# Feed-forward middle of a hybrid decoder step: parts of 4, 6, 6, 6 hidden tiles, four rotating PSUM tiles, and separate buffers for the second row of weight blocks

## The chip, the cores and the metric

The kernel runs on one core of a Trainium2 chip (trn2). The metric is the device time of one execution in microseconds (us). The engines are TensorE (PE, matmul; PEld is its weight load), VectorE (DVE), ScalarE (ACT), GpSimd (POOL) and SyncE (SP), which issues nearly all transfers. Operands lie in SBUF, matmuls add up in PSUM.

## The reference

One layer of a decoder with 1024 channels: half a feed-forward, a mixing stage (a gated convolution beside attention in dilated windows, then an output projection), half a feed-forward again, and a last norm. There are 512 prompt tokens and 8 sample tokens with caches; the kernel treats them together as T = 520 columns. What the change touches is this:

```
def rmsnorm(x, g):
    y = x * lax.rsqrt(jnp.mean(x * x, axis=-1, keepdims=True) + EPS)
    return y * g

def half_ffn(x, g, w1, w3, w2):          # w1, w3: 1024 x 2816, w2: 2816 x 1024
    h = rmsnorm(x, g)
    return x + 0.5 * ((jax.nn.silu(h @ w1) * (h @ w3)) @ w2)

x = half_ffn(x, *ffn1)
...
x = x + jnp.concatenate([y_c, y_a], axis=-1) @ w_out
x = half_ffn(x, *ffn2)
y = rmsnorm(x, norm_final)
```

All of it is float32.

## The kernel before, in words

**Tiling.** x is held transposed: eight tiles X[0] to X[7] of 128 channels x 520 tokens. A matmul takes a block of weights of 128 x 128 and TH = 260 tokens, half of the columns. Float32 accuracy comes from splitting each operand into a rounded part (hi, in the type float32r) and the rest (lo): `mm3` (L119 to L123) issues three matmuls, hi by xh (L121), hi by xl (L122) and lo by xh (L123). `load_w` (L95 to L110) loads weights into `raw` (a ring of four), rounds them to `hi` on ScalarE (L108) and takes `lo` on VectorE (L109); `hi` and `lo` are rings of three in the pool wp.

**One feed-forward** is `ffn` (L226), called for i = 0 before the mixing stage and for i = 1 behind it. The 22 hidden tiles of 128 are done in parts that CUTS names.

1. `x_operand` (L201) scales X by the gain and splits it: f0h, f0l (f1h, f1l) on ScalarE (L135) and VectorE (L136). Squares are summed in `acc`, and `rstd_rows` (L164) turns the sum into `rbc`, the factor of the norm for each token: rounding rhi (ACT L171), matmuls with ones (L178, L179), rv (DVE L182), a logarithm and an exponential on ScalarE, and three VectorE steps to L187. The products are taken of X without the factor, and multiplied by rbc behind the matmul.
2. The first part, tiles 0 to 3, is made by plain products, `gemm`: gate (w1), up (w3), and hh and hl = the rounded hidden tile and its rest (L299, L300). In the first feed-forward the first three products ("early") come from weights w0 that are loaded with x. Beside them `x_sums` (L337) makes seven sums of x's blocks: f0sh and f0sl (f1sh, f1sl).
3. `down` (L395) multiplies the part's hidden tiles by w2 and adds half of the result to X (L404).
4. The other hidden tiles come two at a time from `pair` (L307). It calls `seven` (L354) for w1 and for w3: Strassen's scheme in Winograd's form, seven products of 12 matmuls in place of eight. seven loads two rows of blocks, ra and rb, makes the sums `ws` of them on VectorE (L363 to L366), and rounds them all (L372, L373): ha, hb, hs and la, lb, ls. Products add up in three places of PSUM: px takes five of them, with a copy by ScalarE to `a` or `b` (L380, L384, L388) after most, py one and pw two. The next product into px waits for the copy of px.
5. After each part `down` follows. In the last part of the second feed-forward `finish` and `give` (L796, L820) make the last norm and the output.

**What sets the order.** Nothing here is ordered by hand: a scheduler orders the instructions of each engine by priority and by what is ready, within the buffers that are there. Each engine then does its own row in order. A ring's buffer can only be written again when its last reader is done: that is how pools set the order. SP's queue issues the loads in program order; a load waits until its buffer is free. The mixing stage has an order of its own (ORDER), and the last step of it is the output projection `out_proj`, two passes of four blocks, which ends in X (L747, L748).

**Pools before.** psM gives two PSUM tiles and psA or psB one more; `psum_tile` (L229) goes round these three. The first sums z and the x operands are in one pool xa, the sums xo in another, both on the right side of SBUF; su holds ws, hs, ls. ra and rb share wp's `raw`, ha and hb its `hi`, la and lb its `lo`.

Of the kernel before, what the change touches and what calls it, by code (L numbers as in the profile page):

```python
# [38 lines left out]
CUTS = (0, 4, 14, 22)  # L39
SPLIT = 4  # L40
# [11 lines left out]
def tile_step(ctx: ExitStack, tc: tile.TileContext, xT, w0, w1a, w3a, w2a, w_in, w_out, w1b, w3b, w2b,  # L52
# [173 lines left out]
    def ffn(i, w1, w3, w2, g, psum, finish=None):  # L226
        turn = [0]
# [8 lines left out]
        def hidden(m):  # L236
            at = m - max(c for c in CUTS if c <= m)
            pool = hids[at >= CUTS[1]]
            Hh[m] = pool.tile([P, T], F32R, name=f"hh{at}", tag=f"hh{at}")
            Hl[m] = pool.tile([P, T], F32R, name=f"hl{at}", tag=f"hl{at}")  # L240
            return Hh[m], Hl[m]

        with ExitStack() as st:
            gu = st.enter_context(tc.tile_pool(name=f"gu{i}", bufs=1, reuse_waits="tile"))
            hids = [st.enter_context(tc.tile_pool(name=f"hida{i}", bufs=1, reuse_waits="tile"))]
            with ExitStack() as sx:
                xo = sx.enter_context(tc.tile_pool(name=f"xo{i}", bufs=1, side="right", reuse_waits="tile"))
                with tc.tile_pool(name=f"xa{i}", bufs=1, side="right", reuse_waits="tile") as xa:
                    early = []

                    def start_x():
                        SP.dma_start(gv, gvec)
                        SP.dma_start(X[0][:, TH:], xT[:, 0, TH:])

                    if i == 0:
                        SP.dma_start(X[0][:, :TH], xT[:, 0, :TH])
                        for k in range(0, KD, 2):
                            if k:
                                SP.dma_start(X[k], xT[:, k])
                            early.append(load_w(w0[k // 2], 6, [slice(0, 3), slice(3, 6)] if not k else None, then=start_x if not k else None))  # L260
                            SP.dma_start(X[k + 1], xT[:, k + 1])
                        SP.dma_start(ident, idm)
                    xh, xl, sums = x_operand(xa, f"f{i}", g, i == 0)

                    def norm_tiles():
                        t = psum_tile()
                        return [t[:, h] for h in range(2)]

                    rstd_rows(norm_tiles, sums, D, rbc)
                    if early:  # L270

                        early, ws = [psum_tile() for _ in range(3)], early
                        for k in range(KD):
                            for e, ps in enumerate(early):
                                hi, lo = (t[:, 3 * (k % 2) + e] for t in ws[k // 2])
                                for h in range(2):
                                    c = slice(h * TH, (h + 1) * TH)
                                    mm3(ps[:, h, :TH], hi, lo, xh[k][:, c], xl[k][:, c], k == 0, k == KD - 1)
                    xs = []
                    for m in range(CUTS[1]):  # L280
                        pp = []
                        a = gu.tile([P, T], F32, name="a", tag="a", bufs=2)
                        b = gu.tile([P, T], F32, name="b", tag="b")
                        for w, t in ((w1, a), (w3, b)):
                            if early:

                                A.activation(halves(t), early.pop(0)[:, :, :TH], AF.Copy)
                                pp.append(halves(t))
                                continue
                            hi, lo = load_w(w[m], KD)  # L290
                            ps = psum_tile()
                            gemm(ps, [(hi, lo, 0, KD)], xh, xl)
                            pp.append(ps[:, :, :TH])
                        V.tensor_tensor(halves(a), pp[0], halves(rbc), ALU.mult)
                        A.activation(a, a, AF.Silu)
                        V.tensor_tensor(halves(b), pp[1], halves(rbc), ALU.mult)
                        V.tensor_tensor(b, b, a, ALU.mult)
                        hh, hl = hidden(m)
                        A.activation(hh, b, AF.Copy)  # L299
                        V.tensor_tensor(hl, b, hh.bitcast(F32), ALU.subtract)  # L300

                        xs.append(x_sums(xo, xa, f"f{i}", g, m))
                    down(w2, 0, CUTS[1], Hh, Hl, psum_tile)
                hids.append(st.enter_context(tc.tile_pool(name=f"hidb{i}", bufs=1, reuse_waits="tile")))
                su = sx.enter_context(tc.tile_pool(name=f"su{i}", bufs=2, side="right", reuse_waits="tile"))

                def pair(m):  # L307

                    at, aw, bt = psum_tile(), psum_tile(), psum_tile()
                    a = gu.tile([P, 4, TH], F32, name="a", tag="a", bufs=2)  # L310
                    b = gu.tile([P, 4, TH], F32, name="b", tag="b")
                    x = seven(su, w1, m, xs, at, aw[:, 0, :TH], a)
                    A.activation(a[:, 0:2], a[:, 0:2], AF.Silu)
                    A.activation(a[:, 3], a[:, 3], AF.Silu, scale=-1.0)
                    A.activation(a[:, 2], x, AF.Silu, scale=-1.0)
                    x = seven(su, w3, m, xs, bt, aw[:, 1, :TH], b)
                    V.tensor_tensor(b[:, 0:2], b[:, 0:2], a[:, 0:2], ALU.mult)
                    V.tensor_tensor(b[:, 3], b[:, 3], a[:, 3], ALU.mult)
                    V.tensor_tensor(b[:, 2], x, a[:, 2], ALU.mult)
                    for r, sign in ((0, 1.0), (1, -1.0)):  # L320
                        hh, hl = (halves(t) for t in hidden(m + r))
                        of = b[:, 2 * r:2 * r + 2]
                        A.activation(hh, of, AF.Copy, scale=sign)
                        if r:
                            V.scalar_tensor_tensor(hl, of, sign, hh.bitcast(F32), ALU.mult, ALU.subtract)
                        else:
                            V.tensor_tensor(hl, of, hh.bitcast(F32), ALU.subtract)

                for c0, c1 in zip(CUTS[1:], CUTS[2:]):
                    for m in range(c0, c1, 2):  # L330
                        pair(m)
                    if c1 < KF:
                        down(w2, c0, c1, Hh, Hl, psum_tile)
# [61 lines left out]
    def down(w2, k0, k1, Hh, Hl, psum_tile, finish=None):  # L395
# [18 lines left out]
        if not finish:  # L414
            return
# [522 lines left out]
```

## Time and profile before

| what | value |
|---|---|
| median of three runs | 1035.67 us (1033.27 to 1036.26) |
| the profiled execution | 1036.0 us |
| its span in the trace | 1034.2 us |
| TensorE busy | 996.0 us, 96% of the span, 7897 matmuls recorded |
| VectorE busy | 726.5 us, 70% |
| ScalarE busy | 505.0 us, 49% |
| mean granted TensorE clock | 0.981 of full speed |
| transfers | 136.62 MB, mean 132 GB/s |

The profiled execution is 1.8 us longer than its span, and all places in the trace are given in us from the span's start. Matmuls overlap in the records: one of 128 x 260 at full clock has a duration of 0.28 us and the next one starts 0.12 us later, so the distance of starts is the measure. In brackets stands how long an engine stood idle before an instruction, and what ended that. The first feed-forward fills the time to about 389 us, the mixing stage that to 641, the second feed-forward the rest.

### The profile page before, as it was taken

To read this page: it belongs to the slowest core of one execution; us is meant where nothing else is said; L and a number is where in the kernel's file an instruction comes from. 1 tells how busy PE (TensorE), PEld (TensorE's weight loads), DVE (VectorE), ACT (ScalarE), POOL (GpSimd) and SP (SyncE) were. 2 spreads that over 40 slices of the span, in tenths; PEclk is the share of its full clock that TensorE was granted. 3 is DMA by queue.
4 is the path that set the end of the run, shared out by engine and by line. 5 is a ranking of instruction groups with operands and counts; after the bars stand their busy time and mean duration, and the time that the engine had idled before them with its cause. 6 is when DMAs were issued, how large, how long until landed. Compare 5 with 4: busy or idle time off the path is not lost.

```text
span 1034.2 us, 19174 instructions
## 1 busy us (share of the span) xinstructions
PE 996.0 (96%) x7897; PEld 965.4 (93%) x7897; DVE 726.5 (70%) x1193; ACT 505.0 (49%) x833; POOL 92.2 (9%) x103
## 2 busy tenths in 40 slices
PE   6999999999999999999999998999999999999997
PEld 5999999999999999999999897999998999999897
DVE  6788888436786546667688799797887634788332
ACT  4534565323555436566565545443555422555342
POOL 1000000000000031112022263000000000000022
PEclk6999999999999999999999999999999999999998
DMA  6325434354443445243246665325334233333302
GB/s 208 113 90 186 144 131 140 105 183 156 148 157 125 143 141 173 83 144 129 66 146 222 205 203 184 103 82 184 133 125 151 64 90 113 102 103 103 101 22 83
DMA packets 37912, 136.62 MB, mean 132 GB/s; under 512 B 5760, under 2 KB 8512, under 8 KB 37312
## 3 DMA queue, kind: packets, MB, share of 16 engines
q1 hardware_dynamic: 37824, 135.39, 39.2%
q8 instruction: 62, 1.02, 0.4%
q14 instruction: 26, 0.21, 0.1%
HBM read 131.07 MB, written 37.82 MB: 163 GB/s over the span
## 4 chain that ended last, share of the span: by engine, by line
PE 70%; DVE 15%; DMA 6%; issue 4%; ACT 4%; POOL 1%; SPq 0%; POOLq 0%; DVEq 0%; ACTq 0%
PE ps L121 22%; PE ps L123 21%; PE ps L122 21%; DVE lo L373 3%; DMA raw<-in_w1b 2%; DVE lo L109 2%; DMA raw<-in_w3b 2%; DVE ls L373 1%; ACT hi L108 1%; PE s L568 1%; DMA raw<-in_w1a 1%; DVE ws L364 1%; DVE raw L365 1%; ACT hi L372 1%; DVE ws L363 1%
## 5 line engine op out<-in xcount | busy, mean ns | idle before, releaser
L108 ACT ACTIVATE hi<-raw 128x1024 fp32r<-128x1024 f32 (+3 forms) x136 | 119.1, 878 | 215.6 <-PE ps L122 167.3
L121 PE MATMUL ps<-hh,hi 128*128 128x260 f32 x704 | 200.5, 287 | 4.3 <-ACT hi L108 3.5
L123 PE MATMUL ps<-hh,lo 128*128 128x260 f32 x704 | 200.8, 286 | 1.5 <-DVE lo L109 1.4
L122 PE MATMUL ps<-hl,hi 128*128 128x260 f32 x704 | 199.9, 285 | 0.5 <-DVE hl L300 0.3
L109 DVE TENSOR_TENSOR lo<-raw,hi 128x1024 fp32r<-128x1024 f32 (+3 forms) x136 | 143.6, 1057 | 74.9 <-ACT hi L108 74.0
L121 PEld LDWEIGHTS ps<-hh,hi 128*128 128x128 f32 x704 | 133.5, 191 | 6.8 <-ACT hi L108 4.3
L123 PEld LDWEIGHTS ps<-hh,lo 128*128 128x128 f32 x704 | 134.0, 190 | 3.0 <-DVE lo L109 2.5
L122 PEld LDWEIGHTS ps<-hl,hi 128*128 128x128 f32 x704 | 134.0, 190 | 1.2 <-DVE hl L300 1.2
L121 PE MATMUL ps<-mh,hi 128*128 128x260 f32 x384 | 110.3, 288 | 1.8 <-DVE q L498 1.1
L123 PE MATMUL ps<-mh,lo 128*128 128x260 f32 x384 | 109.3, 285 | 0.3 <-DVE u L619 0.3
L122 PE MATMUL ps<-ml,hi 128*128 128x260 f32 x384 | 109.4, 285 | 0.0
L372 ACT ACTIVATE hi<-raw 128x1024 fp32r<-128x1024 f32 x72 | 75.7, 1053 | 60.8 <-PE ps L122 58.2
L144 POOL TENSOR_TENSOR acc<-acc,sq 128x520 f32<-128x520 f32 (+1 forms) x25 | 38.3, 1530 | 752.9 <-ACT sq L143 748.8
L373 DVE TENSOR_TENSOR lo<-raw,hi 128x1024 fp32r<-128x1024 f32 x72 | 87.5, 1217 | 4.8 <-ACT hi L372 4.8
L372 ACT ACTIVATE hs<-ws 128x1024 fp32r<-128x1024 f32 x72 | 60.5, 840 | 54.0 <-DVE ws L364 48.0
L121 PE MATMUL ps<-f1sh,hi 128*128 128x260 f32 x288 | 82.1, 285 | 3.4 <-DVE X L404 1.2
L121 PE MATMUL ps<-f0sh,hi 128*128 128x260 f32 x288 | 82.2, 286 | 2.0 <-ACT a L384 1.7
L122 PE MATMUL ps<-f0sl,hi 128*128 128x260 f32 x288 | 81.4, 283 | 0.0
L123 PE MATMUL ps<-f1sh,lo 128*128 128x260 f32 x288 | 80.2, 282 | 1.3 <-DVE lo L373 1.2
L122 PE MATMUL ps<-f1sl,hi 128*128 128x260 f32 x288 | 81.3, 283 | 0.0
L123 PE MATMUL ps<-f0sh,lo 128*128 128x260 f32 x288 | 79.6, 282 | 0.0
L404 DVE SCALAR_TENSOR_TENSOR X<-ps,X 128x260 f32<-128x260 f32 x96 | 36.7, 422 | 57.9 <-PE ps L123 57.9
(278 smaller groups left out, 2744.8 us busy)
## 6 DMA issues: line engine op xcount, KB each, us to landing
out_cko<-in_ck SPq DMA_DIRECT2D x16, 1023.0 KB, 7.1
out_cvo<-in_cv SPq DMA_DIRECT2D x16, 1023.0 KB, 7.2
raw<-in_w_in SPq DMA_DIRECT2D x24, 512.0 KB, 3.3
raw<-in_w1b SPq DMA_DIRECT2D x22, 512.0 KB, 3.3
raw<-in_w3b SPq DMA_DIRECT2D x22, 512.0 KB, 3.3
raw<-in_w3a SPq DMA_DIRECT2D x21, 512.0 KB, 3.3
raw<-in_w1a SPq DMA_DIRECT2D x20, 512.0 KB, 3.3
raw<-in_w2a SPq DMA_DIRECT2D x16, 320.0 KB, 3.0
```

Source lines behind the costliest of these rows:

```text
L108: A.activation(hi, raw, AF.Copy)
L109: V.tensor_tensor(lo, raw, hi.bitcast(F32), ALU.subtract)
L121: PE.matmul(out, lhsT=hi, rhs=xh, start=start, stop=False, skip_group_check=more)
L122: PE.matmul(out, lhsT=hi, rhs=xl, start=False, stop=False, skip_group_check=more)
L123: PE.matmul(out, lhsT=lo, rhs=xh, start=False, stop=stop, skip_group_check=more)
L144: G.tensor_tensor(dst[:, c], dst[:, c], sq[:, c], ALU.add)
L363: V.tensor_tensor(s[:, 0], rb[:, :KQ], rb[:, KQ:], ALU.add)
L364: V.tensor_tensor(s[:, 1], s[:, 0], ra[:, :KQ], ALU.add)
L365: V.tensor_tensor(rb[:, :KQ], rb[:, :KQ], ra[:, :KQ], ALU.add)
L372: A.activation(h, f, AF.Copy)
L373: V.tensor_tensor(l, f, h.bitcast(F32), ALU.subtract)
L404: V.scalar_tensor_tensor(X[m][:, c], ps[:, h, :TH], 0.5, X[m][:, c], ALU.mult, ALU.add)
```

## The change

- **Parts.** CUTS is (0, 4, 10, 16, 22): three groups of three pairs instead of one of five and one of four. There is one more `down` pass, with fewer matmuls in each; the number of matmuls is the same.
- **PSUM.** A fourth tile (pool ps4, tag m4) joins the rotation; it is given back before the last `down`. The two tiles psN of the last norm take its place.
- **Second row of blocks.** rb has a ring of two of its own in su, hb and lb have one buffer each there. wp's rings are left to ra, ha, la and w2.
- **Pools of x.** xo goes to the left side, z has its own pool xz, and xa stands alone on the right.
- **Fewer, larger instructions.** px of w1 and of w3 are the two halves of one PSUM tile; py and pw are the two halves of another and are added by one instruction of 520 columns. The hidden tiles are allocated two at a time, and a pair's product, hh and hl are each one instruction of 1040 columns (two of 520 for the last pair of a part). `down` updates X by one instruction of 520. x_sums merges two subtractions. The sign of the second row is turned earlier (`a[:, 3]` by -1 on VectorE, `b[:, 2]` by a copy on ScalarE).
- **Tail.** Of the last `down` three tiles instead of two are done by halves (TAIL), and SPLIT is 1.

```diff
-CUTS = (0, 4, 14, 22)
-SPLIT = 4
+CUTS = (0, 4, 10, 16, 22)
+TAIL, SPLIT = 3, 1
...
         def psum_tile():
             turn[0] += 1
-            pool, tag = (psum, "m3") if turn[0] % 3 == 0 else (psM, "mm")
+            pools = [(p, "m4") for p in more] + [(psM, "mm"), (psM, "mm"), (psum, "m3")]
+            pool, tag = pools[(turn[0] - 1) % len(pools)]
...
-                xo = sx.enter_context(tc.tile_pool(name=f"xo{i}", bufs=1, side="right", reuse_waits="tile"))
-                with tc.tile_pool(name=f"xa{i}", bufs=1, side="right", reuse_waits="tile") as xa:
+            xo = st.enter_context(tc.tile_pool(name=f"xo{i}", bufs=1, reuse_waits="tile"))
+            more.append(sx.enter_context(tc.tile_pool(name=f"ps4{i}", bufs=1, space=PSUM)))
+            with tc.tile_pool(name=f"xa{i}", bufs=1, side="right", reuse_waits="tile") as xa, \
+                    tc.tile_pool(name=f"xz{i}", bufs=2, side="right", reuse_waits="tile") as xz:
...
+            def pair(m, last):
+                px, pa, pb = psum_tile(), psum_tile(), psum_tile()
...
+                x = seven(su, w1, m, xs, px[:, 0, :TH], pa[:, :, :TH], a)
...
+                x = seven(su, w3, m, xs, px[:, 1, :TH], pb[:, :, :TH], b)
+                hh, hl = (t.rearrange("p r (h n) -> p (r h) n", h=2) for t in hidden(m))
+                A.activation(b[:, 2], x, AF.Copy, scale=-1.0)
+                for of in (slice(0, 2), slice(2, 4)) if last else (slice(0, 4),):
+                    V.tensor_tensor(b[:, of], b[:, of], a[:, of], ALU.mult)
+                    A.activation(hh[:, of], b[:, of], AF.Copy)
+                    V.tensor_tensor(hl[:, of], b[:, of], hh[:, of].bitcast(F32), ALU.subtract)
...
             preload()
+            sx.close()
+            more.clear()
             down(w2, CUTS[-2], KF, Hh, Hl, psum_tile, finish)
...
-    def seven(pool, w, m, xs, ps, pw, out):
+    def seven(pool, w, m, xs, px, pyw, out):
+        py, pw = pyw[:, 0], pyw[:, 1]
-        ra, rb = (wp.tile([P, KD, P], F32, name="raw", tag="raw", bufs=4) for _ in range(2))
+        ra = wp.tile([P, KD, P], F32, name="raw", tag="raw", bufs=4)
+        rb = pool.tile([P, KD, P], F32, name="rb", tag="rb")
...
-        ha, hb = (wp.tile([P, KD, P], F32R, name="hi", tag="whi") for _ in range(2))
-        la, lb = (wp.tile([P, KD, P], F32R, name="lo", tag="wlo") for _ in range(2))
+        ha = wp.tile([P, KD, P], F32R, name="hi", tag="whi")
+        la = wp.tile([P, KD, P], F32R, name="lo", tag="wlo")
+        hb, lb = (pool.tile([P, KD, P], F32R, name=n, tag=n, bufs=1) for n in ("hb", "lb"))
...
         product(px, hb, lb, 2, False)
         A.activation(out[:, 2], px, AF.Copy)
         product(pw, hs[:, 2], ls[:, 2], 1, False)
-        V.tensor_tensor(out[:, 3], out[:, 2], out[:, 3], ALU.add)
+        V.scalar_tensor_tensor(out[:, 3], out[:, 2], -1.0, out[:, 3], ALU.mult, ALU.subtract)
         product(px, hb[:, KQ:], lb[:, KQ:], 5, False)
-        V.tensor_tensor(out[:, 1], pw, out[:, 1], ALU.add)
+        V.tensor_tensor(out[:, 0:2], pyw, out[:, 0:2], ALU.add)
```

Three places show how the rows of the engines change. A number behind a name only tells buffers of one name apart; lines of the changed kernel are one higher here.

TensorE at the first norm: ps_223 to ps_225 are the early products before, ps_229 to ps_231 in the changed kernel; rhi by ones_r is the norm's matmul. Before:

```order
L121 MATMUL ps_224<-f0h5_172,hi_135 128x260
L122 MATMUL ps_224<-f0l5_173,hi_135 128x260
L123 MATMUL ps_224<-f0h5_172,lo_136 128x260
L178 MATMUL ps_209<-rhi_205,ones_r_78 128x260
L121 MATMUL ps_223<-f0h0_150,hi_114 128x260
L122 MATMUL ps_223<-f0l0_151,hi_114 128x260
L123 MATMUL ps_223<-f0h0_150,lo_115 128x260
```

With the change:

```order
L122 MATMUL ps_231<-f0h7_186,hi_149 128x260
L123 MATMUL ps_231<-f0l7_187,hi_149 128x260
L124 MATMUL ps_231<-f0h7_186,lo_150 128x260
L179 MATMUL ps_215<-rhi_211,ones_r_78 128x260
L122 MATMUL ps_480<-f0h0_156,hi_475 128x260
```

Before, the norm's matmul stands behind 36 matmuls of one early product and ahead of the other two products; now it stands behind all 144 matmuls of the three, and a later product follows it.

ScalarE at the end of the output projection, where the second feed-forward's operand f1h is made from X (hi is a rounding of weights, sq a square). Before:

```order
L143 ACTIVATE sq_7514<-X4_68 128x520
L108 ACTIVATE hi_7547<-raw_7546 128x1024
L143 ACTIVATE sq_7517<-X5_69 128x520
L108 ACTIVATE hi_7602<-raw_7601 128x1024
L143 ACTIVATE sq_7520<-X6_70 128x520
L108 ACTIVATE hi_7678<-raw_7677 128x1024
L135 ACTIVATE f1h0_7472<-X0_64,gv_74 128x520
L135 ACTIVATE f1h1_7476<-X1_65,gv_74 128x520
```

With the change:

```order
L109 ACTIVATE hi_7255<-raw_7254 128x512
L136 ACTIVATE f1h0_7416<-X0_64,gv_74 128x520
L141 ACTIVATE acc_75<-X0_64 128x520
L136 ACTIVATE f1h1_7420<-X1_65,gv_74 128x520
L144 ACTIVATE sq_7449<-X1_65 128x520
L109 ACTIVATE hi_7289<-raw_7288 128x512
L136 ACTIVATE f1h2_7424<-X2_66,gv_74 128x520
```

Before, all eight f1h stand behind the last squares and the roundings of three later tiles of weights; now each stands behind its own X tile, among the roundings for the output projection.

TensorE inside a pair, where the fourth product into px (of hb, the second row) follows the third (of hs). Before, with ps_1253 the px:

```order
L123 MATMUL ps_1253<-f0sh3_728,ls_1272 128x260
L121 MATMUL ps_1255<-f0sh0_389,hi_1384 128x260
L122 MATMUL ps_1255<-f0sl0_390,hi_1384 128x260
L121 MATMUL ps_1253<-f0sh0_389,hi_1267 128x260
L122 MATMUL ps_1253<-f0sl0_390,hi_1267 128x260
```

With the change, with ps_2075 the px:

```order
L122 MATMUL ps_2075<-f0sh3_726,hs_2210 128x260
L123 MATMUL ps_2075<-f0sl3_727,hs_2210 128x260
L124 MATMUL ps_2075<-f0sh3_726,ls_2211 128x260
L122 MATMUL ps_2075<-f0sh0_394,hb_2208 128x260
L123 MATMUL ps_2075<-f0sl0_395,hb_2208 128x260
```

Before, two matmuls of another product stand between the two; at this place of the changed kernel none does.

## Rows read from the trace of the kernel before

**Rows 1.** Page: span, and the granted clock in 40 slices (tenths).

```profile
span 1034.2 us, 19174 instructions
...
PEclk6999999999999999999999999999999999999998
```

**Rows 2.** Stretches: from:to, length, busy us (matmuls) by engine, clock, DMA share, GB/s.

```profile
67.00:92.00 25.00, 24.00 (x194) 23.20 (x193) 18.61 (x34) 8.20 (x12) 0.00 (x0) 1.00 0.57 190
...
205.00:255.00 50.00, 50.00 (x419) 50.00 (x418) 23.68 (x39) 13.38 (x18) 0.00 (x0) 1.00 0.53 175
...
92.00:388.60 296.60, 291.43 (x2377) 287.59 (x2376) 197.95 (x301) 138.15 (x226) 11.96 (x8) 0.99 0.42 143
719.00:1016.00 297.00, 288.44 (x2347) 283.89 (x2346) 191.52 (x294) 138.04 (x226) 9.09 (x6) 0.99 0.31 100
...
641.00:651.00 10.00, 5.25 (x23) 4.85 (x22) 9.96 (x14) 7.07 (x11) 1.53 (x2) 0.66 0.47 159
```

**Rows 3.** TensorE's timeline and its waits (us, times, longest): copies of px.

```profile
118.37 0.28 PE L122 MATMUL ps<-f0sl,hi 128*128 128x260 f32 x1
118.89 0.39 PE L121 MATMUL ps<-f0sh,hi 128*128 128x260 f32 x1 [0.24 <-ACT a L384]
...
PE ps L121 <- ACT a L384: 1.7, 7, 0.2
...
797.58 0.28 PE L123 MATMUL ps<-f1sh,lo 128*128 128x260 f32 x1
798.34 0.39 PE L121 MATMUL ps<-f1sh,hi 128*128 128x260 f32 x1 [0.48 <-ACT a L388]
```

**Rows 4.** TensorE's timeline and stretches: two ends of parts.

```profile
200.11 0.39 PE L121 MATMUL ps<-hh,hi 128*128 128x260 f32 x1 [0.70 <-ACT hi L108]
...
345.16 0.39 PE L121 MATMUL ps<-hh,hi 128*128 128x260 f32 x1 [1.03 <-ACT hi L108]
...
335.00:351.00 16.00, 14.24 (x98) 13.32 (x97) 7.03 (x10) 5.09 (x7) 0.00 (x0) 0.89 0.50 165
347.20:350.50 3.30, 3.30 (x17) 3.30 (x16) 0.00 (x0) 0.00 (x0) 0.00 (x0) 0.50 1.25 459
```

**Rows 5.** Timelines of TensorE, ScalarE and VectorE: start of the second feed-forward.

```profile
640.83 0.28 PE L123 MATMUL ps<-Yh,lo 128*128 128x260 f32 x1
644.02 0.51 PE L121 MATMUL ps<-f1h,hi 128*128 128x260 f32 x1 [2.90 <-ACT f1h L135]
...
643.25 5.05 ACT L135 ACTIVATE f1h<-X,gv 128x520 fp32r<-128x520 f32 x8
...
643.45 1.07 DVE L748 TENSOR_TENSOR X<-X,t 128x520 f32<-128x520 f32 x1
```

**Rows 6.** Timelines of TensorE and VectorE, and one stretch: head and first part.

```profile
23.35 0.58 PE L178 MATMUL ps<-rhi,ones_r 128*128 128x260 f32 x1 [2.17 <-ACT rhi L171]
...
27.84 0.76 DVE L182 TENSOR_SCALAR rv<-ps 128x260 f32<-128x260 f32 x2 [3.81 <-PE ps L179]
...
31.45 0.70 DVE L187 SCALAR_TENSOR_TENSOR rbc<-rq,rbc 128x520 f32<-128x520 f32 x1
...
35.62 1.22 DVE L109 TENSOR_TENSOR lo<-raw,hi 128x1024 fp32r<-128x1024 f32 x1
...
71.53 0.70 DVE L300 TENSOR_TENSOR hl<-b,hh 128x520 fp32r<-128x520 f32 x1 [0.71 <-ACT hh L299]
...
32.10:72.20 40.10, 39.18 (x322) 38.37 (x321) 37.22 (x54) 21.32 (x24) 0.00 (x0) 1.00 0.39 124
```

**Rows 7.** VectorE's waits in 715 to 805, loads (KB, us to landing), one stretch.

```profile
DVE ws L363 <- DMA raw<-in_w3b: 6.7, 4, 2.8
...
raw<-in_w1b SPq DMA_DIRECT2D x22, 512.0 KB, 3.3
...
92.00:190.00 98.00, 96.59 (x792) 95.18 (x791) 80.78 (x122) 55.70 (x97) 0.00 (x0) 1.00 0.42 143
```

More of the change, by code (lines that the diff above doesn't have):

```diff
@@ L238, in hidden @@
             pool = hids[at >= CUTS[1]]
[L239 to L243, printed above, removed]
+            h, l = (pool.tile([P, 2, T], F32R, name=f"h{x}{at}", tag=f"h{x}{at}") for x in "hl")
+            for r in range(2):
+                Hh[m + r], Hl[m + r] = h[:, r], l[:, r]
+            return h, l
+        with ExitStack() as st, ExitStack() as sx:
@@ L244, in ffn @@
             gu = st.enter_context(tc.tile_pool(name=f"gu{i}", bufs=1, reuse_waits="tile"))
             hids = [st.enter_context(tc.tile_pool(name=f"hida{i}", bufs=1, reuse_waits="tile"))]
-            with ExitStack() as sx:
-                xo = sx.enter_context(tc.tile_pool(name=f"xo{i}", bufs=1, side="right", reuse_waits="tile"))
-                with tc.tile_pool(name=f"xa{i}", bufs=1, side="right", reuse_waits="tile") as xa:
[L249 to L333, printed above, removed]
@@ L334, in ffn @@
+            for c0, c1 in zip(CUTS[1:], CUTS[2:]):
+                for m in range(c0, c1, 2):
+                    pair(m, m == c1 - 2)
+                if c1 < KF:
+                    down(w2, c0, c1, Hh, Hl, psum_tile)
             preload()
+            sx.close()
+            more.clear()
             down(w2, CUTS[-2], KF, Hh, Hl, psum_tile, finish)
     def x_sums(pool, tmp, name, col, k):
-        z = tmp.tile([P, 8, TH], F32, name=f"{name}z", tag="z", bufs=2)
+        z = tmp.tile([P, 8, TH], F32, name=f"{name}z", tag="z")
@@ L404, in update, with whole @@
             V.scalar_tensor_tensor(X[m][:, c], ps[:, h, :TH], 0.5, X[m][:, c], ALU.mult, ALU.add)
-        for m in range(KD - 2 if finish else KD):
+        def whole(m):
             ws = parts(m)
@@ L409, in down @@
             gemm(ps, ws, Hh, Hl)
-            for h in range(2):
-                update(m, ps, h)
+            V.scalar_tensor_tensor(halves(X[m]), ps[:, :, :TH], 0.5, halves(X[m]), ALU.mult, ALU.add)
             if finish:
                 finish(m, None)
+        for m in range(KD - TAIL if finish else KD):
+            whole(m)
         if not finish:
             return
-        ws = [parts(m) for m in (KD - 2, KD - 1)]
+        ws = [parts(m) for m in range(KD - TAIL, KD)]
         for h in range(2):
-            ps = psum_tile()
-            gemm(ps, ws[0], Hh, Hl, [h])
-            update(KD - 2, ps, h)
-            finish(KD - 2, h)
+            for m in range(KD - TAIL, KD - 1):
+                ps = psum_tile()
+                gemm(ps, ws[m - KD + TAIL], Hh, Hl, [h])
+                update(m, ps, h)
+                finish(m, h)
             ps = psum_tile()
             if not h:
-                gemm(ps, ws[1], Hh, Hl, [0])
+                gemm(ps, ws[-1], Hh, Hl, [0])
                 update(KD - 1, ps, 0)
@@ L790, in tile_step @@
             out_proj(4, r2)
-    with ExitStack() as st_f, tc.tile_pool(name="psB", bufs=1, space=PSUM, reuse_waits="tile") as psB:
+    with tc.tile_pool(name="psB", bufs=1, space=PSUM, reuse_waits="tile") as psB, ExitStack() as st_f:
         TF = TH // 4
@@ L805, in finish @@
                 part["p"] = st_f.enter_context(tc.tile_pool(name="fp", bufs=1, side="right", reuse_waits="tile"))
+                part["ps"] = st_f.enter_context(tc.tile_pool(name="psN", bufs=1, space=PSUM))
                 part["sq"] = part["p"].tile([P, T], F32, name="fsq")
@@ L808, in finish @@
             c = slice(h * TH, (h + 1) * TH)
-            ps = psB.tile([P, 512], F32, name=f"nps{h}", tag=f"n{h}")
+            ps = part["ps"].tile([P, 512], F32, name=f"nps{h}", tag=f"n{h}")
             A.activation(sq[:, c], X[m][:, c], AF.Square)
@@ L822, in give @@
             fp, c = part["p"], slice(h * TH, (h + 1) * TH)
-            both = [ps, psB.tile([P, 512], F32, name="nps0", tag="n0")] if h else [ps]
+            both = [ps, part["ps"].tile([P, 512], F32, name="nps0", tag="n0")] if h else [ps]
             for p in both:
```

76 lines of the change are left out of this document (64 added, 12 removed).

## Prediction, made before the changed kernel was run

> **What bounds the kernel now.** I read the page's totals first. TensorE's row of clocks is full in nearly all of the 40 slices [rows 1]; the question is therefore not which engine is the bound but where TensorE stands still or runs at half clock. I read that from the table of stretches, by one rule. In 205 to 255 us nothing waits: 419 matmuls touch 50.00 us, two of them at the edges, so one takes 50.00/417 = 0.120 us. Any other stretch has lost its length minus (its matmuls - 2) x 0.120. By that rule the middle of the first feed-forward (92 to 388.6) lost 11.8 us, that of the second (719 to 1016) 15.8 us, the beginning of the second (641 to 651) 7.5 us, and the end of the first feed-forward's first part (67 to 92) 2.0 us [rows 2]. Everything else, the mixing stage above all, is nearly the same on TensorE in both programs. So the change can touch about 37 us in the feed-forwards, besides the head (the first 32 us).
>
> Then I looked at what each loss is. **(a) px.** seven() sums five products in one PSUM tile and copies it to SBUF four times; the next product has to wait for the copy. With two other matmuls put between, the next one starts 0.52 us after its forerunner, with 0.24 idle; seven such waits behind one line are counted in the first feed-forward. With none between, 0.76 us and 0.48 idle [rows 3]. Beyond a pitch, and with 0.1 us for a slow second matmul, that is 0.5 and 0.74 us. **(b) The ends of parts.** There the down product waits for the rounded w2 weights, which wait for a buffer of the ring of three: 0.70 us at 200.11 and 1.03 us at 345.16. After the second the granted clock was 0.50 for 3.3 us (half of 2.4 GHz), after the first it was not; the whole end at 335 to 351 us cost 16.00 - 96 x 0.120 = 4.5 us, the half clock some 3.3/2 = 1.7 of it [rows 4]. **(c) The second start.** The last product of the output projection begins at 640.83, the first of the second feed-forward at 644.02. Its operand f1h was only made in a block of eight from 643.25, although seven of the eight X tiles were done before the last one at 643.45 + 1.07 = 644.5 [rows 5]. **(d) The head.** The norm's matmul starts at 23.35; VectorE reads its result at 27.84 and has rbc at 31.45 + 0.70 = 32.15 (4.3 us later); the last hidden rest of the first part is done at 72.2. Of these 40.1 us VectorE works 37.22: it is the bound there [rows 6].
>
> **The change, part by part** (sums against the profiled execution's 1036.0 us; the median of the runs shown is 1035.67, 0.3 us less).
>
> *A. Head and first part, -1.5 us.* All three early tiles (144 matmuls) stand before the norm's matmul, instead of 36. They can start where the 36 did, at about 8.3. At full pitch the 144 end at 8.3 + 17.2 = 25.5; the sum's rounding stands behind two weight roundings in ScalarE's queue, so the norm is done at about 27 and rbc at 27 + 4.3 = 31.5. If the clock stays at half (0.22 us a matmul) until 26.3, as it did, 86 are done by then, the rest ends at 33.2 and rbc is at 37.4. I take 34. Behind rbc VectorE's list is shorter by three lo subtractions of 1.22 us [rows 6], which now stand ahead of the norm, and about 1.5 us of smaller ones (merged x_sums and one more lo): 40.1 - 5.2 = 34.9. The last rest comes at 66.4 to 72.3, in the middle 68.9. But TensorE has only 30 down matmuls left to do before it, so it idles some us there and I count 1.7 us for a half clock after it; 162 matmuls are left (19.4 us): 68.9 + 1.7 + 19.4 = 90.0, and half of the 2.0 us that this stretch loses now: about 91 against 92.3. Bounds: 66.4 + 19.4 + 1 = 86.8 (-5.5) and 72.3 + 1.7 + 19.4 + 2 = 95.4 (+3).
>
> *B and D. The two middles, +0.8 and -3.2 us.* The number of matmuls is the same (7842 in both programs). With four rotating tiles and one px tile for w1 and w3, the scheduler's order shows, per feed-forward: about five waits inside a group with nothing between (5 x 0.74), one with one and one with two between (0.6 + 0.5): 4.8 us; one end per part where the last products have nothing to be mixed with, three of 1.0 to 1.4 us: 3.4; the first down product waiting for the last pair's rounding, halved by `last`, three times 0.8: 2.4; and lateness of weights, where I put 2, a share of the waits on loads in the second half [rows 7]. Sum 12.6. The wait for w2 [rows 4] is not in it: three of its tiles are rounded before a part ends now, because rb, hb and lb have left the rings. What covers an evacuation now is only a 0.12 us matmul per place; where even that is gone I have priced it at 0.74. 12.6 against 11.8 and 15.8 gives the two terms. The clock is not lost in it, since 0.70 us of waiting kept it. Bounds: the px waits hidden as well as today and ends at 0.7 us: 8 (-4 and -7.2); twelve waits instead of seven, or half clocks at two ends, 3.4 more to 5 more (+5 and +3).
>
> *C. The second start, -5.7 us.* ScalarE now makes each f1h right behind its X tile, so the eight are spread over the output projection; the last is ready near 644.5 + 0.65, its rest near 646, and TensorE has 44 matmuls (5.3 us from 641) that need no f1h7. Of the 7.5 us some 1.8 stay, for the norm and a slow first group. Bounds: 0.2 left (-7.3), or ScalarE's extra work in front of the w_out roundings holding the last output tiles (-3).
>
> *E. Tail, -0.3 us.* Three last tiles by halves with SPLIT 1; the final chain behind the last matmul is unchanged. Bounds 0 and -0.5.
>
> VectorE's instructions fall from 1195 to 1080, ScalarE's rise from 802 to 810; both lie beside matmuls in the middles and I count them at nothing there: in 92 to 190 VectorE works 80.78 of 98.00 us [rows 7]. The 282 transfers are the same.
>
> Sum: -1.5 + 0.8 - 5.7 - 3.2 - 0.3 = -9.9, so 1036.0 - 9.9 = **1026 us**.
>
> **The rivals.**
>
> *More than that, 1012 us.* The early block runs at full clock, and the four tiles hide px: every term at its better bound, -5.5 - 4 - 6.8 - 7.2 - 0.5 = -24. For it: TensorE is dense earlier in the head. Against it: the order shows the bare places. Chance 0.16.
>
> *No change, 1036 us: the clock at the ends of parts.* Six ends with waits of 1.0 to 1.4 us instead of four. Of the two ends shown, the longer wait lost the clock, the shorter one not [rows 4]; if each new end loses it, 6 x 1.7 = 10.2 us eat the gain: 1026 + 10 = 1036. It decides at a wait between 0.70 and 1.03 us at a part's end. For it: my own price of an end is over 1.0. Against: the wait for w2, the cause of both, is gone. The Trainium skill, page "TensorE: Matmul & The Clock Gate", section "A second HAM failure mode: psum-queue depth-cycling", speaks against rotating through banks: a kernel that cycled through PSUM banks had its matmul groups broken by many very short idle times, and its clock swung between both levels. By it the change would lose clock also at the places inside the parts; the trace of before does not bear that out, since px waits of 0.24 and 0.48 us left the mean granted clock of 92 to 388.6 at 0.99 [rows 2]. Chance 0.14.
>
> *Slower, 1044 us: the raw second block is late.* rb has a ring of two and hb, lb one buffer each. The load into an rb can only start when VectorE has read the one before, and takes 3.3 us; VectorE's next instruction in order is the sum that needs it. Today 4 such waits of up to 2.8 us stand in one stretch of the second half [rows 7]. VectorE has 80.78 us of work per 790/168 = 4.7 pairs, 17.2 us a pair, where TensorE needs 168 x 0.120 = 20.2. So it decides at 3.0 us of waiting per pair: at 4.0, 1 us for each of 18 pairs, +18: 1026 + 18 = 1044. For it: an rb of w3 frees only right ahead of the next w1's. Against: VectorE loses over a tenth of its instructions. Chance 0.13.
>
> *The change doesn't do what it says*: the order of f1h shows it does; 0.01.
>
> **How the numbers follow.** My forecast has 0.56, with a range of its own of 1018 to 1034. A measurement of this kernel can tell about 0.3% (3.1 us) from no change. Faster: 0.56 + 0.16, and 0.01 of the rest; same 0.14; slower 0.13. The range goes from 1012 (the larger gain, with about a twentieth below) to 1037 (no change, all but the slower case).
>
> **What would show it.** C: no TensorE idle over 1 us near 641 to 647, and f1h single in ScalarE's row. Ends of parts: no wait on hi at L109, clocks of 1.00 there. Head: rbc near 34 and the last rest near 69. Middles: waits of 0.4 to 0.5 us behind `a` and `b` copies. I am wrong if the six ends show 0.50 clocks, or if VectorE waits on loads of rb by over 3 us a pair.

## The result, and the profile after

The changed kernel takes **1053.32 us** (median of four, 1048.93 to 1054.22) against 1035.97 for the kernel before: ratio 1.0168, 95% interval 1.0141 to 1.0195. It is slower by some 17 us, where 10 us less were forecast. The profiled execution is the quickest of the four, 1048.93 us, 12.9 more than the 1036.0 of before; the other three, at 1052.6 to 1054.2, had a mean granted clock of 0.983 instead of its 0.988. The trace therefore shows 13 of the 17 us.

The page of the changed kernel, the lines that answer to [rows 1]:

```profile
span 1047.2 us, 19070 instructions
...
PEclk9989999999999999999999999999989999999998
```

The stretches, for [rows 2], with the columns as there; the first is the head and the second the end of the first part, the next two are the middles, then the second start, and the last two are the pieces of the middles at half clock:

```profile
4.60:26.10 21.50, 19.03 (x146) 17.86 (x146) 19.54 (x25) 14.01 (x21) 4.22 (x3) 1.00 0.76 271
55.10:88.60 33.50, 27.68 (x197) 26.55 (x196) 27.11 (x38) 12.84 (x15) 0.00 (x0) 0.85 0.60 204
88.60:397.00 308.40, 295.06 (x2376) 288.48 (x2375) 197.04 (x251) 141.71 (x228) 9.70 (x7) 0.99 0.39 130
725.90:1029.70 303.80, 291.19 (x2340) 285.32 (x2339) 189.43 (x243) 140.41 (x228) 6.96 (x6) 0.99 0.28 89
649.70:659.70 10.00, 7.95 (x61) 7.37 (x61) 9.70 (x11) 5.46 (x9) 2.60 (x2) 1.00 0.36 119
123.40:126.80 3.40, 2.99 (x14) 3.00 (x15) 1.63 (x2) 0.95 (x4) 0.00 (x0) 0.50 0.10 35
758.20:765.00 6.80, 6.22 (x27) 5.93 (x28) 5.66 (x9) 4.19 (x7) 0.00 (x0) 0.50 0.23 77
```

By the prediction's rule (length minus matmuls less two, by 50/417 us) the middles now lose 308.4 - 2374 x 50/417 = 23.7 us and 303.8 - 2338 x 50/417 = 23.5 us, where they lost 11.8 and 15.8. Cut behind the last down matmul of each first part, at the places that the rows name, and for the tail at the last norm's first matmul, the spans of both profiles compare like this:

| piece | before | after | difference | forecast |
|---|---|---|---|---|
| head and first part | 91.8 | 88.6 | -3.2 | -1.5 |
| first middle | 296.8 | 308.5 | +11.7 | +0.8 |
| mixing stage, to the last output matmul | 252.3 | 252.7 | +0.4 | 0 |
| second start, to the first down matmul | 54.0 | 49.3 | -4.6 | -5.7 |
| first part's down in the second feed-forward | 24.2 | 26.8 | +2.6 | (in -5.7) |
| second middle | 296.8 | 303.9 | +7.1 | -3.2 |
| tail | 18.5 | 17.4 | -1.1 | -0.3 |

Outside the middles no piece is further from its forecast than the second start with the down behind it, 3.7 us. By the table the middles are 21 us away from it, and one place shows how. These are some of the rows of ScalarE, VectorE and TensorE from 118 to 125 us, put in order of time:

```profile
118.63 1.06 ACT L377 ACTIVATE hb<-rb 128x1024 fp32r<-128x1024 f32 x1 [3.27 <-PE ps L123]
119.72 1.23 DVE L378 TENSOR_TENSOR lb<-rb,hb 128x1024 fp32r<-128x1024 f32 x1 [4.10 <-ACT hb L377]
119.74 0.39 PE L122 MATMUL ps<-f0sh,hb 128*128 128x260 f32 x1 [1.03 <-ACT hb L377]
120.86 1.24 DVE L327 TENSOR_TENSOR b<-b,a 128x1040 f32<-128x1040 f32 x1
121.00 0.39 PE L124 MATMUL ps<-f0sh,lb 128*128 128x260 f32 x1 [0.75 <-DVE lb L378]
122.13 1.07 ACT L328 ACTIVATE hh<-b 128x1040 fp32r<-128x1040 f32 x1 [2.17 <-DVE b L327]
123.38 0.38 ACT L392 ACTIVATE a<-ps 128x260 f32<-128x260 f32 x1
123.81 0.59 PE L122 MATMUL ps<-f0sh,hb 128*128 128x260 f32 x1 [1.33 <-ACT a L392]
```

ScalarE cannot round into the one buffer hb until TensorE has done with the block before; TensorE's next product in order needs just that hb, waits 1.03 us for it and 0.75 us for lb. VectorE had stood 4.10 us before lb, so the last product of the pair (L327) is late behind it, so hh is late behind that on ScalarE, and the copy of px (L392) stands in ScalarE's row behind hh. TensorE waits for it a third time, 1.33 us; from 123.4 us on, within this wait, the clock is at 0.50 for 3.4 us. Together that is 5.2 us lost at one hand-over from one block to the next. The same chain stands at 757 us. There the clock falls earlier, at 758.2, with the second of the waits (1.03 and 0.75 us), and stays at half for 6.8 us; the copy is late by 0.48 us.

What TensorE waits for in the second middle, and ScalarE's and VectorE's waits there (us, times, longest):

```profile
PE ps L122 <- ACT hs L377: 2.7, 2, 1.5
PE ps L122 <- ACT hb L377: 2.1, 2, 1.1
PE ps L122 <- ACT b L389: 1.9, 4, 0.5
PE ps L122 <- ACT hi L109: 1.6, 2, 0.8
PE ps L124 <- DVE lb L378: 1.4, 2, 0.8
...
ACT hb L377 <- PE ps L123: 18.6, 11, 3.3
...
DVE lb L378 <- ACT hb L377: 26.0, 12, 4.1
...
DVE ws L367 <- DMA rb<-in_w3b: 10.1, 6, 3.3
```

VectorE waits 10.1 us on loads of rb (6.7 in [rows 7], over a shorter stretch), but 26.0 on hb. The wait for w2 at L109, which [rows 4] had at 0.70 and 1.03 us, is still there, 0.81 us at two of the three ends.

### The profile page after: what moved, and what is told of

The parts are those of the page before. It is cut to its first block, busy times and chain, and to the rows that moved or that the text cites. A ratio compares the mean times of both kernels' runs of the same rounds, so it can differ in the third digit from the quotient of the medians.

```text
span 1047.2 us, 19070 instructions
## 1 busy us (share of the span) xinstructions
PE 997.3 (95%) x7897; PEld 963.8 (92%) x7897; DVE 729.4 (70%) x1078; ACT 513.4 (49%) x841; POOL 90.4 (9%) x104
## 5 line engine op out<-in xcount | busy, mean ns | idle before, releaser
L109 ACT ACTIVATE hi<-raw 128x768 fp32r<-128x768 f32 (+2 forms) x136 | 118.8, 876 | 176.3 <-PE ps L123 142.1
L110 DVE TENSOR_TENSOR lo<-raw,hi 128x768 fp32r<-128x768 f32 (+2 forms) x136 | 141.0, 1038 | 39.5 <-ACT hi L109 37.2
L378 DVE TENSOR_TENSOR lb<-rb,hb 128x1024 fp32r<-128x1024 f32 x36 | 44.1, 1224 | 48.9 <-ACT hb L377 48.9
L122 PEld LDWEIGHTS ps<-mh,hi 128*128 128x128 f32 x384 | 72.3, 188 | 3.5 <-issue 2.4
L414 DVE SCALAR_TENSOR_TENSOR X<-ps,X 128x520 f32<-128x520 f32 x61 | 42.6, 698 | 46.5 <-PE ps L124 46.5
L124 PEld LDWEIGHTS ps<-mh,lo 128*128 128x128 f32 x384 | 72.3, 188 | 1.5 <-DVE u L626 0.5
L123 PEld LDWEIGHTS ps<-ml,hi 128*128 128x128 f32 x384 | 72.3, 188 | 1.3 <-issue 0.9
L378 DVE TENSOR_TENSOR ls<-ws,hs 128x1024 fp32r<-128x1024 f32 x72 | 67.4, 953 | 1.9 <-ACT hs L377 1.9
L378 DVE TENSOR_TENSOR lo<-raw,hi 128x1024 fp32r<-128x1024 f32 x36 | 44.0, 1222 | 32.3 <-ACT hi L377 32.2
L122 PE MATMUL ps<-f1sh,hs 128*128 128x260 f32 x216 | 62.1, 288 | 3.7 <-ACT hs L377 2.7
```

The costliest lines, as they stand in the source:

```text
L109: A.activation(hi, raw, AF.Copy)
L110: V.tensor_tensor(lo, raw, hi.bitcast(F32), ALU.subtract)
L122: PE.matmul(out, lhsT=hi, rhs=xh, start=start, stop=False, skip_group_check=more)
L123: PE.matmul(out, lhsT=hi, rhs=xl, start=False, stop=False, skip_group_check=more)
L124: PE.matmul(out, lhsT=lo, rhs=xh, start=False, stop=stop, skip_group_check=more)
L378: V.tensor_tensor(l, f, h.bitcast(F32), ALU.subtract)
```

## The experiments

The kernels were timed beside the kernel before, up to four of them on one chip; differences between kernels of different groups are taken from their ratios to it, with 1035 us for 1. S, R, G, P, F, L, W and D are the theories that the expectations name.

**First four: which part costs.**

e1: hb and lb back in the rings.

```diff
-        hb, lb = (pool.tile([P, KD, P], F32R, name=n, tag=n, bufs=1) for n in ("hb", "lb"))
+        hb = wp.tile([P, KD, P], F32R, name="hi", tag="whi")
+        lb = wp.tile([P, KD, P], F32R, name="lo", tag="wlo")
```

> The changed kernel with hb and lb taken back into the rings of three that ha, la and w2 use (rb keeps its own ring of two). Theory S (the single hb and lb are what costs: ScalarE's rounding into hb waits until TensorE has done the last product of the block before, and what stands behind it on ScalarE and VectorE waits with it): the waits on hb, lb and the copy behind them, about 1.3 + 1.0 + 0.9 + 2.9 us in the first feed-forward's middle and as much in the second's, go: 1053 - 12 = 1041 us, less if w2 now waits for the ring at the ends of parts (about +1 us at each of six). Theory R (the ring of two of rb is what costs, since VectorE stands up to 3.4 us before the first sum of rb until its load lands): the waits on loads stay and the time stays at 1050 to 1054. Theory G (three groups instead of two cost, by their ends and by bare waits for px): 1051 to 1054.

1037.05 us, ratio 1.0020 (1.0002 to 1.0039). 15 us of the 17 go when hb and lb are not single. S holds, with 4 us more than it forecast; R and G fall.

e2: rb back in its ring, hb and lb stay single.

```diff
-        rb = pool.tile([P, KD, P], F32, name="rb", tag="rb")
+        rb = wp.tile([P, KD, P], F32, name="raw", tag="raw", bufs=4)
```

> The changed kernel with rb taken back into the ring of four raw buffers (hb and lb keep their single buffers). Theory R: VectorE's waits on loads of rb (9.4 us in the first middle, 10.1 in the second) shrink to the 5 us of before, and the late hs and ls with them: 1042 to 1046. Theory S: the waits of ScalarE's hb on TensorE stay (12.8 us, eight times, in the first middle): 1050 to 1055. Theory G: 1051 to 1055.

1061.96 us, ratio 1.0274 (1.0231 to 1.0318): outside all three expectations. ScalarE's waits in the first middle show why:

```profile
ACT hb L377 <- PE ps L123: 18.8, 9, 3.6
...
ACT hi L377 <- DMA raw<-in_w1a: 10.1, 3, 6.4
```

The trace is of the slowest execution, 1070.4 us; the other three took 1061.6 to 1062.0. The wait for TensorE is 18.8 us, where the change has 12.8 in the same middle, and one on loads of the first row comes besides, up to 6.4 us. Two reasons fit, and no run tells them apart: an rb that waits for its hb holds a raw buffer that ra and w2 need; and TensorE's order is another one, with a single matmul between two uses of hb at 10 of 30 places, where the change has 3 (this count is explained at e8). Either way rb's own ring made the single hb cheaper; it was not the cost.

e3: both edits.

> The changed kernel with rb, hb and lb all back in the shared rings, as before the change; parts of 4, 6, 6, 6, four PSUM tiles, joined px and the new places of x stay. Theories S and R together: the second row's lateness was the cost, so both middles come to about 13 us lost instead of 24: 1053 - 22 = 1031. Theory G: the groups and the px waits stay, and w2 waits for the ring at six ends again: 1048 to 1055.

1033.86 us, ratio 0.9988 (0.9969 to 1.0008). Near S and R together, but still no gain, though head, second start and tail keep theirs. The middles lose 15.5 and 15.3 us here, summed over TensorE's late starts.

e4: the kernel before, only `CUTS = (0, 4, 10, 16, 22)`.

> The kernel before with nothing changed but the parts, 4, 6, 6, 6. Theory G: two more ends of parts (0.70 to 1.03 us of waiting for w2, 1.5 to 4.6 us lost with a half clock) and two more starts of groups: 1036 + 8 to 15 = 1044 to 1051. Theories S and R: the parts are not the cost; two more ends at 1.5 to 4.5 us: 1039 to 1045.

1029.11 us, ratio 0.9938 (0.9918 to 0.9959). A miss by all theories: the parts alone are a gain of 6 us. The last end of a part in the first feed-forward, which answers to the one at 345.16 in [rows 4]:

```profile
356.56 0.39 PE L121 MATMUL ps<-hh,hi 128*128 128x260 f32 x1 [0.34 <-ACT hi L108]
...
349.00:365.00 16.00, 15.50 (x123) 14.70 (x122) 9.11 (x16) 7.38 (x10) 0.00 (x0) 1.00 0.45 144
```

The wait is 0.34 us instead of 1.03 and the clock stays at 1.00. This end loses 1.5 us (16.00 - 121 x 0.120), where that one lost 4.5. All six ends of e4 wait 0.34 us, and its middles have no half clock, where the trace of before has 3.4 us of it in each.

**Second four: why the rings alone are not enough, and whether a single buffer always costs.**

e5: hb and lb with `bufs=2` in their own pool, rb in the raw ring to make room.

> The changed kernel with two own buffers each for hb and lb; to make room, rb is back in the ring of four raw buffers. Theory S (one buffer is the cost): the waits on hb and lb go, as in e1, and the time is that of e3, 1032 to 1037 us. Rival: that rb shares raw buffers is itself slow (e2 was 1062): then 1042 to 1062. If only the single hb made e2 slow (rb is not read out until hb is free, so raw buffers stay taken), it is 1032 to 1037.

1029.81 us, ratio 0.9967 (0.9948 to 0.9986), 2 us below the forecast. A second buffer takes the cost away, and rb in the ring does no harm then.

e6: pair, seven and x_sums of before in the changed kernel, rb, hb, lb in the rings.

```diff
-                px, pa, pb = psum_tile(), psum_tile(), psum_tile()
+                at, aw, bt = psum_tile(), psum_tile(), psum_tile()
...
-                x = seven(su, w1, m, xs, px[:, 0, :TH], pa[:, :, :TH], a)
+                x = seven(su, w1, m, xs, at, aw[:, 0, :TH], a)
```

> The changed kernel with pair, seven and x_sums as before the change (rb, hb, lb in the shared rings; px and py in one PSUM tile, two pw in another; additions and products in the small pieces of before); the four rotating PSUM tiles, the parts, the places of x and the tail stay. Theory P (the joined px/pw layout and the wide last steps leave the copies of px bare): the middles come from e3's 15.5 and 15.4 us lost to e4's 10.9 and 8.0, so 1034 - 12 = 1022. Theory F (the fourth tile is what changes the order to bare waits): 1031 to 1036 as in e3.

1021.73 us, ratio 0.9886 (0.9858 to 0.9914). P holds in its size, F falls: 11 us (0.9988 to 0.9886) lie in the new pair, seven and x_sums. Whether bare copies are the reason, as P says, is asked at e13.

e7: as e6, the fourth tile given back behind the first down.

```diff
             down(w2, 0, CUTS[1], Hh, Hl, psum_tile)
+            s4.close()
+            more.clear()
```

> As e6, but the fourth PSUM tile is given back behind the first down, so that the pairs rotate through three tiles. Both theories: the middles are those of e4 (10.9 and 8.0 us lost), and the head (-3.5 us), the second start (-0.3 to -1.8) and the tail (-1) are the changed kernel's: 1029 - 5 = 1024 us.

**1018.68 us**, ratio 0.9856 (0.9837 to 0.9876): 15 us under the kernel before, 5 under the forecast of both theories, and the shortest median here. How much of it the three tiles give is not shown: e7's trace is 3.5 us shorter than e6's, but only 0.7 us of that lie in the middles, where the two differ in tiles.

e8: e4 with single hb and lb.

> The kernel before with parts 4, 6, 6, 6 (e4) and hb and lb in one own buffer each, nothing else. Theory S: the single buffers cost here too, by ScalarE's wait for TensorE in each pair: 1029 + 12 to 20 = 1041 to 1049. If they only cost together with the joined px, 1027 to 1032.

1021.70 us, ratio 0.9881 (0.9859 to 0.9902). A single buffer is no cost here but a gain of 6 us over e4: theory S falls as it stood. For the gain the trace shows that no wait for w2 (L108) is left at the ends, behind which e4's middles lose 3.4 and 4.1 us. That the cost stays away goes with TensorE's order. In the changed kernel the third block of a group follows the second like this (the number tells the blocks apart):

```
L122 MATMUL ps_996<-f0sh3_726,hb_1129 128x260
L123 MATMUL ps_996<-f0sl3_727,hb_1129 128x260
L124 MATMUL ps_996<-f0sh3_726,lb_1130 128x260
L122 MATMUL ps_1237<-f0sh0_394,hb_1253 128x260
L123 MATMUL ps_1237<-f0sl0_395,hb_1253 128x260
L124 MATMUL ps_1237<-f0sh0_394,lb_1254 128x260
```

Nothing but one matmul with lb lies between the last use of one hb and the first of the next, while rounding and rest take 1.06 + 1.23 us, 19 matmuls. I counted the 30 hand-overs inside groups in TensorE's order: in the changed kernel 12 have at most 13 matmuls between, in e8 six have 13 and 24 have 37 or more. That is theory D: a single buffer costs where the order hands it over at once, and hides where 37 matmuls (4.4 us) lie between.

**Third four: theory D.**

e9: the change whole, with the edit of e7.

> The changed kernel whole, with single hb and lb and the joined px, but the fourth PSUM tile is given back behind the first down, so that the pairs rotate through three. Theory D (what a single hb costs depends on how many matmuls TensorE's order puts between the last one that reads the old hb and the first that reads the new one; rounding and rest take 1.06 + 1.22 us, 20 matmuls): of the 30 hand-overs inside groups the changed kernel has 14 with at most 13 matmuls between, this one has 4, and most others 25 or more. 16 us went with all of them in e1, so 14 become 4: 1053 - 12 = 1041, and some 3 us less from the three tiles (e6 to e7): 1036 to 1042. Theory S (a single buffer costs whatever the order): 1049 to 1054.

1057.78 us, ratio 1.0237 (1.0202 to 1.0273). A miss, and by the same count the hand-overs did get longer (the change's count in this expectation is 12, not 14). TensorE's waits in its first middle:

```profile
PE ps L122 <- ACT b L390: 5.8, 7, 1.3
PE ps L122 <- ACT b L386: 3.6, 4, 1.1
PE ps L122 <- ACT b L326: 2.7, 2, 1.4
PE ps L122 <- ACT a L386: 2.4, 2, 1.3
```

No wait on hb or lb is left. Copies of px take their place, 1.1 to 1.4 us long at the worst. With three tiles the next pair's px is the same tile, and two of the waits are for the last copy of the pair before (L326); the others are inside a pair, and in this order two products into one place of PSUM stand back to back 28 times, 11 times in the change. So D is right about hb and wrong about the time: the joined px is a cost of its own.

e10: e6 with the change's own buffers for rb, hb and lb.

> e6 (old pair, four rotating tiles) with the changed kernel's own buffers: rb a ring of two, hb and lb single. Theory D: the order leaves at most 15 matmuls at 18 of the 30 hand-overs (1 to 3 at five of them), so it costs as in the changed kernel, some 1.2 us each: 1022 + 15 to 22 = 1037 to 1044. Theory P (single buffers only cost together with the joined px layout): 1015 to 1023.

1032.26 us, ratio 0.9980 (0.9955 to 1.0005), 10 us over e6 (at most 15 matmuls at 14 hand-overs; the 18 above is a miscount). P falls. D holds in kind, below its range: 0.7 us a hand-over instead of 1.2.

e11: e7 with single hb and lb. e12: that with rb's own ring besides.

> e7 (old pair, three tiles in the pairs, four in front of them) with hb and lb single, rb in the ring of raw buffers. Theory D: at 24 of the 30 hand-overs 37 matmuls (4.4 us) lie between, so the single buffers hide, and they leave the rings to ha and w2 as in e8, which was 7 us under e4: 1019 - 7 = 1012. Theory S: 1019 + 12 = 1031.

> As e11 with rb in its own ring of two besides. Theory D: 13 matmuls at 8 hand-overs, 37 or more at the others, as good as e11: 1011 to 1015. Theory R (rb's ring of two makes VectorE wait for loads): 1018 to 1025.

1018.75 us, ratio 0.9863 (0.9826 to 0.9899), and 1020.00, ratio 0.9867 (0.9828 to 0.9906). With 37 matmuls between at most places, single buffers cost no more than can be told beside e7 (0.9856), as D says. The further gain that D forecast, as of e8 over e4, did not come in the time, and both runs lie above D's range; e12's number is one that R gave, but it lies no further from e11's than the intervals allow. In the traces a part of the gain is there: the middles of e11 are 3.6 us shorter than those of e7, with no wait for w2 left, but outside them e11 has 3.4 and 6.8 us at half clock (575.8 and 688.4) that e7's trace has not.

**Last three: what in the new pair costs.**

e13: e3 with px and py in one tile and the two pw in another, as before; the rest of the new pair stays.

```diff
         product(py, ha[:, KQ:], la[:, KQ:], 0, True)
+        V.tensor_tensor(out[:, 0], py, out[:, 0], ALU.add)
...
-        V.tensor_tensor(out[:, 0:2], pyw, out[:, 0:2], ALU.add)
+        V.tensor_tensor(out[:, 1], pw, out[:, 1], ALU.add)
```

> e3 (the changed kernel, rb, hb, lb in the shared rings, four rotating tiles) with the places in PSUM of before: px and py of one block in one tile, both pw in a third, so py and pw are added apart. The wide last steps, the copy of the sign and the order of the sums stay. Theory L (the layout costs: products of one tile stand back to back in TensorE's order at 40 places of e3, at 10 of this kernel): 1034 - 12 = 1022 us, as e6. Theory W (the wide last steps of a pair cost): 1031 to 1036.

1026.78 us, ratio 0.9936 (0.9916 to 0.9956), between the two forecasts. What went with the layout is this, in e3 (a place of it, and the sum for the first middle):

```profile
202.03 1.06 ACT L378 ACTIVATE hi<-raw 128x1024 fp32r<-128x1024 f32 x1 [1.69 <-PE ps L123]
203.14 0.39 PE L122 MATMUL ps<-f0sh,hi 128*128 128x260 f32 x1 [1.03 <-ACT hi L378]
...
PE ps L122 <- ACT hi L378: 3.1, 3, 1.0
```

In e13 no wait of TensorE on these roundings is left. It is the hand-over again, now in the ring of three: at three places of each middle e3's order puts one matmul between the last reader of a buffer and the first reader of what comes into it, where e13's puts 13 or more inside a group. So the layout costs, but with rings not by bare copies: TensorE's waits on copies in the first middle are 1.8 us in e3 and 3.3 in e13.

e14: e3 with the last steps of every pair in two halves.

```diff
-                for of in (slice(0, 2), slice(2, 4)) if last else (slice(0, 4),):
+                for of in (slice(0, 2), slice(2, 4)):
```

> e3 with the last steps of every pair in two halves of 520 columns, the joined layout kept. Theory L: 1031 to 1036, the order on TensorE is the same. Theory W: 1034 - 8 to 12 = 1022 to 1026.

1032.81 us, ratio 1.0010 (0.9989 to 1.0031).

e15: the change with the edit of e13 alone.

> The whole change, own buffers and four rotating tiles, with only the places in PSUM of before (as e13). Theory L with theory D: the layout's 12 us go, the hand-overs of the single hb stay short (at most 15 matmuls at 13 of 30): 1053 - 12 = 1041 or, with e10's order, down to 1032. Theory W: 1050 to 1054.

1042.36 us, ratio 1.0085 (1.0058 to 1.0111). L holds in kind: the layout is 5 of the 11 us with rings (0.9988 to 0.9936) and 9 us in the whole change (1.0168 to 1.0085); narrower last steps alone gain nothing (e14). Against e13, this run gives the price of the own buffers once more: 15 us (0.9936 to 1.0085), with at most 15 matmuls at 13 hand-overs. The other 5 us between e13 and e6 (the copy of the sign, the order of the sums, the wide steps with the old layout) stay open; in the traces they lie in the second middle, 293.5 us against 288.1.

## Why the prediction was wrong

**A, head: right, size within its bounds.** The early block ran at full clock from the start (1.00 in 4.6 to 26.1 us), the better of the two cases; rbc was at 32.65, and TensorE waited for the last rest, as the sum had it:

```profile
25.98 0.28 PE L179 MATMUL ps<-rhi,ones_r 128*128 128x260 f32 x1
...
31.95 0.70 DVE L188 SCALAR_TENSOR_TENSOR rbc<-rq,rbc 128x520 f32<-128x520 f32 x1
...
66.17 0.58 PE L123 MATMUL ps<-hl,hi 128*128 128x260 f32 x1 [2.05 <-DVE hl L306]
```

The last rest came at 66.2, just ahead of the 66.4 to 72.3 of the forecast. But the clock was at 0.50 from 61.9 to 72.2 us (it makes the 0.85 of the second stretch above), and the 6.0 us of it behind the last rest cost 3.0, where the sum had 1.7. -3.2 us, forecast -1.5: the rest 2.7 us ahead of the middle of its bounds made up for that, so the size is in part luck. The forecast's 92.3 us for the kernel before is 91.8 by the cut of the table; and in the case at half clock 18.0/0.22 gives 82 matmuls, not 86, so that its rbc would come about half a us later.

**C, second start: right in the mechanism, then given back.** The idle time of 2.90 us [rows 5] became 1.04, a little over the 1 us that the forecast named as its sign, and each f1h stands by its own X tile:

```profile
649.76 0.28 PE L124 MATMUL ps<-Yh,lo 128*128 128x260 f32 x1
651.08 0.36 PE L122 MATMUL ps<-f1h,hi 128*128 128x260 f32 x1 [1.04 <-DVE t L754]
...
641.98 0.73 ACT L136 ACTIVATE f1h<-X,gv 128x520 fp32r<-128x520 f32 x1 [1.83 <-DVE X L755]
...
703.28 0.51 PE L122 MATMUL ps<-hh,hi 128*128 128x260 f32 x2 [1.65 <-ACT hh L305]
705.18 0.39 PE L124 MATMUL ps<-hh,lo 128*128 128x260 f32 x1 [1.39 <-DVE lo L110]
```

That gave 4.6 of 5.7 us. But 2.6 went in the down behind it (last two lines): TensorE is there before the last hidden tile hh of the first part and before a rest of w2. In VectorE's row the product that hh is made from, and that rest, stand behind the rests of x's sums, 2.0 us each. I had seen this stall in the first feed-forward and left it out in the second. With it the term is -2.0 us, outside its bounds of -7.3 to -3.

**B and D, the middles: the step that failed.** It is the line "lateness of weights, where I put 2", with the px waits beside it. I summed how much later than 0.120 us TensorE's matmuls start, with each wait the slow starts that follow it. Waits on hb, lb, hs and ls then took 7.1 us in the first middle and 8.8 in the second, not 2; the copies of px, with the half clock behind them, 10.4 and 9.1 instead of 4.8. I had read in the order which products of px stand bare, but not what stands between two uses of the single hb. Most late copies waited the 0.48 us that I had priced, nine in both middles, at 1.0 us each instead of 0.74; the two in the chain above (L392, at 123.8 and 761.3 us) took 3.2 and 2.7, because ScalarE's and VectorE's rows ahead of them stand on hb and the clock falls. Only the waits of the down products came near the 3.4 + 2.4 forecast for the ends, at 6.2 and 5.4 us, and that is luck: 4.3 and 4.2 of it are the wait for w2, which I took for gone (0.81 us at two ends in each middle, L109 above).

**The rivals.** The slower one came nearest, 1044 us at a chance of 0.13, yet for another reason: it charged loads of rb and decided at 3.0 us of VectorE's waiting on them per pair. In the second middle VectorE waited 10.1 us on rb (above), in the first this:

```profile
DVE ws L367 <- DMA rb<-in_w3a: 9.4, 6, 3.4
...
DVE ws L367 <- DMA rb<-in_w1a: 5.0, 4, 1.8
```

By 9 pairs each that is 1.6 and 1.1 us, so by its own rule it should not have happened; e1 shows hb and lb, and e2 that without rb's own ring the change is worse still. The clock at the ends: there were no 0.50 clocks at any end of a part in the middles; they began at 123.4 and 758.2 us, at the waits of a hand-over. The rule of the Trainium skill ("TensorE: Matmul & The Clock Gate", section "A second HAM failure mode: psum-queue depth-cycling") would have made the four rotating tiles the cause. The runs here don't bear it out: with the old pair, four tiles against three (e6, e7) make 0.7 us in the two middles, at mean granted clocks of 0.989 and 0.991 of the whole; with the new pair three tiles are slower than four (e9); and the change's profiled execution has 0.988 where the kernel before has 0.981.

**The parts** I counted as neutral or a little worse (one more end, 1.0 to 1.4 us each). Alone they gain 6 us (e4). With the old pair the changed kernel is 12 and 15 us under the kernel before (e6, e7); in the change the cost of the buffers and the layout lies over it.

## What to carry to other kernels

A ring, above all one with one buffer, is priced by the matmuls that the order puts between the last reader of the old content and the first reader of the new one, against the time to refill it; count that distance at every hand-over, in the order after the change. Where several accumulations share one PSUM tile, the order changes with it, so count again: the hand-overs in all rings (e3 against e13), and the products that stand back to back (e9). And a wait in an in-order row is paid again by what is queued behind it: price the chain, not the first wait.

## What was not expected of the hardware

Short waits close together went with a fall of the clock where a longer one alone did not. At 119 to 124 us three waits of 1.03, 0.75 and 1.33 us, with TensorE working between, went with a granted clock of 0.50 from 123.4 us on for 3.4 us, and at 757 us two of 1.03 and 0.75 us with one from 758.2 us on for 6.8 us; after a single wait of 1.53 us, on hs at 773.58, the clock stayed at 1.00. And one kernel's executions differ by 5 us with a mean granted clock of 0.988 or 0.983. Which places account for that is not shown, since only one execution was traced.
